# Hybrid decoder block on one core: first weights split in three, a third raw-weight buffer, later squares

## The chip, the cores and the metric

One NeuronCore of one Trainium2 chip runs the whole kernel in one launch. The metric is the device time of one execution in microseconds (us); the number for the kernel before is the median of three executions. One further execution was recorded by the hardware profiler, and every row below comes from that one.

## What is computed

The reference is one decoder block (batch 1, 512 tokens, model width 1024, depth 1). The whole change lies in its first lines, the first norm and the first columns of the combined projection:

```python
h = rms_norm(x, attn_norm_g[i])
u = h @ w_in[i]
u_sb, u_rw, u_gate = jnp.split(u, [SB_COLS, SB_COLS + RW_COLS], axis=-1)
q, k, v = jnp.split(u_sb.reshape(bsz, seq, 3 * SB_HEADS, SB_HEAD_DIM), 3, axis=2)
o_sb = stick_breaking_attention(q, k, v).reshape(bsz, seq, SB_WIDTH)
o_rw = rwkv7_time_mix(u_rw, ...)
```

After it come the gated merge of the two branches, a squared-ReLU MLP, the gated per-layer embedding and a final norm. All inputs and outputs are float32.

## The kernel before

**Numbers in two halves.** Products keep float32 accuracy by splitting each operand in a rounded high part and the low rest: `x = hi + lo`. A product is then three matmuls (`mm3`, lines 186 to 194): weight-hi by x-hi (L191), weight-hi by x-lo (L192), weight-lo by x-hi (L193), each 128 contraction rows by 512 tokens. The split of a weight tile costs one cast on ScalarE (ACT) for `w_hi` and one subtraction on VectorE (DVE) for `w_lo`: lines 221 and 222 for the very first tiles, 175 and 176 for all later ones.

**Weights in units.** All weights lie in memory as units of 128 x 1024 float32 (512 KB). The list `seq` fixes the order in which they are used. `load_to` (L157 to L162) starts a unit's load from the SyncE queue (SP) into a raw buffer `w_raw`, of which there are two; a buffer comes free when the subtraction that makes `w_lo` has read it. `fetch_to` then issues the cast and the subtraction into one of three pairs `w_hi`, `w_lo`; a pair comes free when TensorE (PE) has done the last matmul with it. Units are counted from 0 here: units 0 and 1 are the first q and k columns (head pair 0), unit 2 the first v columns, units 3 to 5 those of head pair 1, and so on.

**The start.** PE first runs matmuls on a zeroed tile `warm` (L335, L336) whose result nobody reads. Meanwhile x, transposed to eight tiles of 128 features by 512 tokens (256 KB each), comes in; `first_x(k)` (L349 to L355) loads tile k, scales it by the norm's gain into `h_hi` on ACT (L353) and makes `h_lo` on DVE (L354). The gain lies in `cols`, a small table of per-feature vectors. `first_weights` (L344 to L347) loads and splits a part of unit 0 or 1. The first loop on PE (L528 to L530) goes over the eight tiles k and for each does six matmuls, three with unit 0 and three with unit 1: 48 in all. Then comes the v projection (24 matmuls, unit 2), and after it the projections of head pair 1 (24 each).

**The norm comes late.** The division by the root mean square is not applied to x but to the results: `sum_squares` (L224 to L234) squares each x tile on ACT and adds it up in `ssum` on DVE; one float32 matmul with a constant matrix sums over partitions (L263, within `rstd_of`), and ACT and DVE turn that into `rs` (L251 to L258). `projected` multiplies q, k and v by `rs` on DVE (`qT` L394, `kT` L406, `vT` L414) and splits them; PE transposes `vT` (L421) and multiplies q with k (`scores`, L458 to L460). So the first scores wait for `ssum`, L263, `rs`, `qT` and the splits of q and k, in that order.

**What sets the order.** A scheduler puts the instructions in order for each engine at build time; on the chip each engine keeps that order. `tc.issue_after(i)` pins what is issued inside it behind instruction i on the same engine. DMA loads share eight completion semaphores: a load that reuses one waits in the queue until the load before it on that semaphore has landed.

Of the kernel before, what the change touches and what calls it, by code (L numbers as in the profile page):

```python
# [10 lines left out]
F32 = mybir.dt.float32  # L11
F32R = mybir.dt.float32r
BF16 = mybir.dt.bfloat16
AF = mybir.ActivationFunctionType
# [4 lines left out]
P = 128  # L19
T = 512  # L20
D = 1024
KT = D // P
# [63 lines left out]
def tile_block(ctx: ExitStack, tc: tile.TileContext, xT, xt, pT, wts, lora, cols_d, gfin_d, consts_d, out, dbg=None):  # L86
    nc = tc.nc
    act, dve, pool, pe, sync = nc.scalar, nc.vector, nc.gpsimd, nc.tensor, nc.sync
# [17 lines left out]
    cols = const.tile([P, NCOLS], F32, name="cols")  # L106
# [12 lines left out]
    def col(name, i):  # L119
        return cols[:, COLS[name] + i:COLS[name] + i + 1]  # L120
# [35 lines left out]
    def load_to(n):  # L156
        while len(loaded) < min(n, len(seq)):  # L157
            i = len(loaded)
            loaded.append(None)
            if seq[i][0] != U_FF2:  # L160
                loaded[i] = wpool.tile([P, 1024], F32, name="w_raw", bufs=2)
                sync.dma_start(out=loaded[i], in_=unit(i))  # L162

    def fetch_to(n, ahead=0):
# [59 lines left out]
    def sum_squares(pool_, src, k, ssum):  # L224

        if k == 0:
            act.activation(out=ssum, in_=src, func=AF.Square)
            return
        sq = pool_.tile([P, T], F32, name="sq", bufs=2)[:, 0:src.shape[-1]]
        act.activation(out=sq, in_=src, func=AF.Square)  # L230
        if k == 1:
            dve.scalar_tensor_tensor(out=ssum, in0=sq, scalar=NORM_EPS * D / P, in1=ssum, op0=ALU.add, op1=ALU.add)
        else:
            dve.tensor_tensor(out=ssum, in0=ssum, in1=sq, op=ALU.add)  # L234
# [42 lines left out]
    with ExitStack() as sA:  # L277
# [43 lines left out]
        with ExitStack() as s1:  # L321
# [10 lines left out]
            warm = p1.tile([P, T], BF16, name="warm", tag="sp")  # L332
            pool.memset(warm, 0.0)
            ps = ps_z()
            for _ in range(12):  # L335
                pe.matmul(ps, warm[:, 0:P], warm, start=True, stop=True)  # L336
            sync.dma_start(out=cols, in_=cols_d)
            ssum = p1.tile([P, T], F32, name="ssum", tag="wl")

            raws = [wpool.tile([P, 1024], F32, name="w_raw", bufs=2) for _ in range(2)]  # L340
            first_w = [[wpool.tile([P, 1024], F32R, name=n) for n in ("w_hi", "w_lo")] for _ in range(2)]
            xs_in = {}

            def first_weights(i, part):  # L344
                cs = slice(part * 512, part * 512 + 512)
                sync.dma_start(out=raws[i][:, cs], in_=unit(i)[:, cs])
                split(first_w[i][0][:, cs], first_w[i][1][:, cs], raws[i][:, cs])  # L347

            def first_x(k):  # L349
                x_in = p1.tile([P, 2, T], F32, name="x_in", tag=("sp", "sph", "spl", "wh")[k // 2]) if k % 2 == 0 else xs_in[k - 1][0]  # L350
                sync.dma_start(out=x_in[:, k % 2, :], in_=xT[:, k, :])
                xs_in[k] = x_in, x_in[:, k % 2, :]
                act.activation(out=h_hi[:, k, :], in_=xs_in[k][1], func=AF.Copy, scale=col("attn_g", k))  # L353
                dve.scalar_tensor_tensor(out=h_lo[:, k, :], in0=xs_in[k][1], scalar=col("attn_g", k), in1=r32(h_hi[:, k, :]),  # L354
                                         op0=ALU.mult, op1=ALU.subtract)  # L355


            first_weights(0, 0)
            first_x(0)
            first_weights(1, 0)  # L360
            for k in range(1, 4):
                first_x(k)
            first_weights(0, 1)
            first_weights(1, 1)
            for k in range(4, KT):
                first_x(k)
            loaded.extend(raws)
# [2 lines left out]
                ready[seq[i]] = [tuple(first_w[i])]  # L370
            fetch_to(3)

            for k in range(KT):
                sum_squares(p1, xs_in[k][1], k, ssum)
            sync.dma_start(out=cst, in_=consts_d[:, 0:NCONST])
            first = p1.tile([P, 4 * P], F32, name="first", tag="sums", bufs=1)
            sync.dma_start(out=first, in_=consts_d[:, NCONST:NCONST + 4 * P])
# [1048 lines left out]
```

## Time and profile before

| what | value |
|---|---|
| median of three executions | 870.2 us (869.28 to 870.54) |
| the profiled execution, its own time | 869.75 us |
| its span, first to last instruction | 867.7 us |
| PE busy in the span | 851.4 us (98%) |
| DVE busy | 678.1 us (78%) |
| ACT busy | 448.6 us (52%) |
| loads of weight units, median from issue to landing | 3.5 us |
| loads of x tiles, median from issue to landing | 5.7 us |

The profile lists every instruction with its engine, source line, start and duration. A timeline merges neighbours of one line: "x3" is three instructions, and the second number then spans all of them. What stands in square brackets is the idle time of the engine just before, and what ended it. PE matmuls are pipelined: one of 512 columns is listed with about 0.39 us, but the next one starts about 0.23 us after it, so the pace is read from start to start, or from the count in a window. SPq and PEq are the queues that issue for an engine. Idle time of an engine that nobody waits for costs nothing.

### The profile page before, as it was taken

The numbers are of one execution on the slowest core, as the hardware profiler recorded it, in microseconds if no ns is written. First come the engines' busy times: TensorE is split into PE (matmuls) and PEld (weight loads), VectorE is DVE, ScalarE is ACT, GpSimd is POOL, SyncE is SP. The second block draws the span as 40 slices with busy tenths as digits, with TensorE's granted clock in tenths as the row PEclk, the third lists the DMA queues.
The fourth block names the chain that finished last, engine by engine and source line by source line (L and its number), as shares of the span: only waits on it lengthen the run. The fifth ranks groups of instructions, "written<-read, shape, count | busy, mean of one in ns | idle before, by whom it ended". The sixth has DMA issues, their size and how long they took to land.

```text
span 867.7 us, 13424 instructions
## 1 busy us (share of the span) xinstructions
PE 851.4 (98%) x5182; PEld 686.8 (79%) x5182; DVE 678.1 (78%) x1228; ACT 448.6 (52%) x703; POOL 80.4 (9%) x138
## 2 busy tenths in 40 slices
PE   8999999999999999999999999999999999999996
PEld 5778787877777777777888888888888888888885
DVE  7899987896979888776754789858985987697767
ACT  6888887744335343534424464344434543453744
POOL 1432431002302111020000000000000000000000
PEclk9999999999999999999999999999999999999999
DMA  7212212221121224437935621531252034300422
GB/s 269 98 49 66 82 62 85 74 97 51 62 87 57 80 73 153 141 116 258 318 121 181 232 73 38 182 120 49 83 184 98 25 127 164 98 1 0 170 73 98
DMA packets 32272, 95.32 MB, mean 110 GB/s; under 512 B 3664, under 2 KB 3664, under 8 KB 32208
## 3 DMA queue, kind: packets, MB, share of 16 engines
q1 hardware_dynamic: 32208, 94.46, 32.6%
q8 instruction: 41, 0.67, 0.3%
q14 instruction: 23, 0.19, 0.1%
HBM read 83.96 MB, written 10.49 MB: 109 GB/s over the span
## 4 chain that ended last, share of the span: by engine, by line
PE 81%; DVE 10%; ACT 4%; issue 1%; DMA 1%; SPq 0%; POOL 0%; POOLq 0%; DVEq 0%; ACTq 0%
PE ps_m L191 13%; PE ps_m L193 13%; PE ps_m L192 13%; PE ps_m L206 9%; PE ps_m L207 9%; PE ps_m L208 9%; DVE w_lo L176 2%; PE ps_g L817 1%; PE ps_o L497 1%; PE ps_g L193 1%; PE ps_c L935 1%; PE ps_s L944 1%; PE ps_g L191 1%; PE ps_g L192 1%; PE ps_g L906 1%
## 5 line engine op out<-in xcount | busy, mean ns | idle before, releaser
L175 ACT CAST w_hi<-w_raw 128x1024 fp32r<-128x1024 f32 x94 | 99.0, 1053 | 170.4 <-PE ps_m L192 110.8
L176 DVE TENSOR_TENSOR w_lo<-w_raw,w_hi 128x1024 fp32r<-128x1024 f32 x94 | 115.1, 1225 | 37.6 <-ACT w_hi L175 37.2
L191 PE MATMUL ps_m<-h_hi,w_hi 128*128 128x512 f32 x320 | 130.6, 410 | 0.9 <-ACT h_hi L353 0.9
L192 PE MATMUL ps_m<-h_lo,w_hi 128*128 128x512 f32 x320 | 128.0, 400 | 0.0
L193 PE MATMUL ps_m<-h_hi,w_lo 128*128 128x512 f32 x320 | 127.5, 399 | 0.0
L191 PE MATMUL ps_m<-hx,w_hi 128*128 128x512 f32 x256 | 99.6, 390 | 0.4 <-ACT hx L1049 0.4
L192 PE MATMUL ps_m<-hx,w_hi 128*128 128x512 f32 x256 | 99.6, 390 | 0.0
L193 PE MATMUL ps_m<-hx,w_lo 128*128 128x512 f32 x256 | 99.5, 389 | 0.0
L191 PEld LDWEIGHTS ps_m<-h_hi,w_hi 128*128 128x128 f32 x320 | 60.7, 190 | 11.4 <-ACT h_hi L353 1.6
L193 PEld LDWEIGHTS ps_m<-h_hi,w_lo 128*128 128x128 f32 x320 | 60.3, 188 | 11.8
L192 PEld LDWEIGHTS ps_m<-h_lo,w_hi 128*128 128x128 f32 x320 | 60.5, 189 | 11.0 <-DVE h_lo L354 1.1
L191 PEld LDWEIGHTS ps_m<-hx,w_hi 128*128 128x128 f32 x256 | 48.0, 188 | 10.5 <-ACT hx L1049 0.6
L192 PEld LDWEIGHTS ps_m<-hx,w_hi 128*128 128x128 f32 x256 | 48.1, 188 | 10.2 <-DVE hx L1050 0.2
L193 PEld LDWEIGHTS ps_m<-hx,w_lo 128*128 128x128 f32 x256 | 48.0, 188 | 10.0
L207 PE MATMUL ps_m<-w_lo,fS 128*128 128x512 f32 x128 | 49.8, 389 | 0.0
L208 PE MATMUL ps_m<-w_hi,fS 128*128 128x512 f32 x128 | 49.8, 389 | 0.0
L206 PE MATMUL ps_m<-w_hi,fS 128*128 128x512 f32 x128 | 49.8, 389 | 0.0
L1291 POOL TENSOR_SCALAR r<-s 128x1 f32<-128x1 f32 x1 | 0.5, 519 | 478.9 <-DVE t L1271 478.9
L208 PE MATMUL ps_m<-w_hi,fA 128*128 128x512 f32 x96 | 37.4, 389 | 0.0
L207 PE MATMUL ps_m<-w_lo,fA 128*128 128x512 f32 x96 | 37.3, 389 | 0.0
L206 PE MATMUL ps_m<-w_hi,fA 128*128 128x512 f32 x96 | 37.3, 389 | 0.0
L221 ACT CAST fS<-sums 128x256 fp32r<-128x256 f32 (+1 forms) x32 | 19.8, 620 | 33.3 <-DVE sums L1141 33.3
(378 smaller groups left out, 1911.6 us busy)
## 6 DMA issues: line engine op xcount, KB each, us to landing
w_raw<-in_wts_dram SPq DMA_DIRECT2D x98, 512.0 KB, 3.5
gates<-gg SPq DMA_DIRECT2D x16, 256.0 KB, 2.1
x_in<-in_xT_dram SPq DMA_DIRECT2D x8, 256.0 KB, 5.7
tmp<-gates SPq DMA_DIRECT2D x8, 256.0 KB, 4.0
upsb<-tmp SPq DMA_DIRECT2D x8, 256.0 KB, 3.5
ga<-upsb SPq DMA_DIRECT2D x8, 256.0 KB, 5.4
gb<-gates SPq DMA_DIRECT2D x8, 256.0 KB, 5.4
xs<-in_xt_dram SPq DMA_DIRECT2D x4, 512.0 KB, 5.9
```

The lines of the kernel that those rows point to most:

```text
L175: act.copy(out=hi, in_=raw)
L176: dve.tensor_tensor(out=lo, in0=raw, in1=r32(hi), op=ALU.subtract)
L191: pe.matmul(ps, wh, xh[:, k, t], start=first, stop=False)
L192: pe.matmul(ps, wh, xl[:, k, t], start=False, stop=False)
L193: pe.matmul(ps, wl, xh[:, k, t], start=False, stop=last)
L206: pe.matmul(ps, xh[:, k + j], wh, start=first and j == 0, stop=False, skip_group_check=True)
L207: pe.matmul(ps, xh[:, k + j], wl, start=False, stop=False, skip_group_check=True)
L208: pe.matmul(ps, xl[:, k + j], wh, start=False, stop=last and j == 1, skip_group_check=True)
L221: act.copy(out=hi, in_=src)
L497: pe.matmul(ps_o[:, j * P:T], vv[:, j, hh, :, :].rearrange("p a d -> p (a d)"), part[:, ZB[j]:ZB[j] + ZN[j]], start=j == 2 and part is wh, ...
L817: last = pe.matmul(ps[rows, k], left[rows, k, :], rhs[rows, k], start=True, stop=True)
L906: pe.matmul(ps[:, j * P:(j + 1) * P], Z[:, hh * 4 + g * 2 + cp, :], MA[:, g * 4 + j, :], start=True, stop=True)
```

## The change

The diff, whole but for the moved line numbers:

```diff
@@ load_to
-                loaded[i] = wpool.tile([P, 1024], F32, name="w_raw", bufs=2)
+                loaded[i] = wpool.tile([P, 1024], F32, name="w_raw", bufs=3)
@@ start of the attention stage
-            for _ in range(12):
+            for _ in range(9):
                 pe.matmul(ps, warm[:, 0:P], warm, start=True, stop=True)
-            sync.dma_start(out=cols, in_=cols_d)
+            act.dma_start(out=cols, in_=cols_d)
-            raws = [wpool.tile([P, 1024], F32, name="w_raw", bufs=2) for _ in range(2)]
+            raws = [wpool.tile([P, 1024], F32, name="w_raw", bufs=3) for _ in range(2)]
-            xs_in = {}
-
-            def first_weights(i, part):
-                cs = slice(part * 512, part * 512 + 512)
+            xs_in, tiles = {}, []
+
+            def first_weights(i, lo, n):
+                cs = slice(lo * P, (lo + n) * P)
                 sync.dma_start(out=raws[i][:, cs], in_=unit(i)[:, cs])
                 split(first_w[i][0][:, cs], first_w[i][1][:, cs], raws[i][:, cs])
@@ first_x
-                act.activation(out=h_hi[:, k, :], in_=xs_in[k][1], func=AF.Copy, scale=col("attn_g", k))
+                with tc.issue_after(tiles[-1]) if tiles else nullcontext():
+                    tiles.append(act.activation(out=h_hi[:, k, :], in_=xs_in[k][1], func=AF.Copy, scale=col("attn_g", k)).ins)
@@ the order of the first loads
-            first_weights(0, 0)
+            first_weights(0, 0, 2)
             first_x(0)
-            first_weights(1, 0)
-            for k in range(1, 4):
-                first_x(k)
-            first_weights(0, 1)
-            first_weights(1, 1)
+            first_weights(1, 0, 2)
+            first_x(1)
+            first_x(2)
+            for i in range(2):
+                first_weights(i, 2, 2)
+            first_x(3)
+            for i in range(2):
+                first_weights(i, 4, 4)
             for k in range(4, KT):
                 first_x(k)
@@ the squares
-            for k in range(KT):
-                sum_squares(p1, xs_in[k][1], k, ssum)
+            for k, behind in enumerate((0, 4, 5, 6, 7, 7, 7, 7)):
+                with tc.issue_after(tiles[behind]):
+                    sum_squares(p1, xs_in[k][1], k, ssum)
@@ kernel
-    nc = bacc.Bacc("TRN2", target_bir_lowering=False, num_devices=1)
+    nc = bacc.Bacc("TRN2", target_bir_lowering=False, num_devices=1, dynamic_dma_scratch_size=2048)
```

In words: three warm matmuls fewer; `cols` is loaded from ACT's queue; units 0 and 1 come in parts of 256, 256 and 512 columns (two, two and four tiles k) instead of two halves; the scaling of tile k is pinned behind that of tile k-1 on ACT, and the squares of tiles 1 to 7 behind the scalings of tiles 4 to 7; a third raw buffer, for which a smaller DMA scratch leaves the room. The output is the same function of the inputs.

Line numbers behind line 350 move up, by 1 at `h_hi` and `h_lo` and by 5 from the squares on. On every engine the order of instructions differs in the first 60 us; behind that PE's is the same, instruction for instruction, and the others differ in a few neighbours.

The loads on the SP queue, from the first on (`w_raw` at L346 are parts of units 0 and 1, `w_raw` at L162 whole units from unit 2 on, `x_in` the tiles of x):

Before:

```order
L337 DMA cols<-in_cols_dram 128x74
L346 DMA w_raw<-in_wts_dram 128x512
L351 DMA x_in<-in_xT_dram 128x512
L346 DMA w_raw<-in_wts_dram 128x512
L351 DMA x_in<-in_xT_dram 128x512 x3
L346 DMA w_raw<-in_wts_dram 128x512 x2
L351 DMA x_in<-in_xT_dram 128x512 x4
L162 DMA w_raw<-in_wts_dram 128x1024
L375 DMA cst<-in_consts_dram 128x584
L377 DMA first<-in_consts_dram 128x512
L162 DMA w_raw<-in_wts_dram 128x1024
```

Now:

```order
L346 DMA w_raw<-in_wts_dram 128x256
L351 DMA x_in<-in_xT_dram 128x512
L346 DMA w_raw<-in_wts_dram 128x256
L351 DMA x_in<-in_xT_dram 128x512 x2
L346 DMA w_raw<-in_wts_dram 128x256 x2
L351 DMA x_in<-in_xT_dram 128x512
L346 DMA w_raw<-in_wts_dram 128x512 x2
L351 DMA x_in<-in_xT_dram 128x512 x4
L162 DMA w_raw<-in_wts_dram 128x1024
L380 DMA cst<-in_consts_dram 128x584
L382 DMA first<-in_consts_dram 128x512
L162 DMA w_raw<-in_wts_dram 128x1024 x3
```

`cols` is gone from this queue, the quarters let x tiles 0 to 2 in with half the weight bytes ahead of them, and the load of unit 3 (the second whole unit) now has the loads of units 4 and 5 right behind it, ahead of `lora_w`.

The subtractions and the norm on DVE, where `rs` is made and q, k and v are scaled (`w_lo` at L176 here are units 3 to 5). Before:

```order
L540 CAST caus_b<-first 128x128
L176 TENSOR_TENSOR w_lo<-w_raw,w_hi 128x1024 x2
L256 SCALAR_TENSOR_TENSOR nt<-nt,ps_z 128x512
L257 SCALAR_TENSOR_TENSOR rs<-nt,rs 128x512
L176 TENSOR_TENSOR w_lo<-w_raw,w_hi 128x1024
L394 SCALAR_TENSOR_TENSOR qT<-ps_m,rs 128x512
L406 TENSOR_TENSOR kT<-ps_m,rs 128x512
L414 TENSOR_TENSOR vT<-ps_z,rs 128x512
```

Now:

```order
L176 TENSOR_TENSOR w_lo<-w_raw,w_hi 128x1024
L234 TENSOR_TENSOR ssum<-ssum,sq 128x512
L176 TENSOR_TENSOR w_lo<-w_raw,w_hi 128x1024 x2
L256 SCALAR_TENSOR_TENSOR nt<-nt,ps_z 128x512
L257 SCALAR_TENSOR_TENSOR rs<-nt,rs 128x512
L399 SCALAR_TENSOR_TENSOR qT<-ps_m,rs 128x512
L411 TENSOR_TENSOR kT<-ps_m,rs 128x512
L419 TENSOR_TENSOR vT<-ps_z,rs 128x512
```

The subtraction of unit 5 stood between `rs` and `qT`; it now stands ahead of `nt`. All eight squares are still added up ahead of it.

The end of the fourth projection on PE (unit 3, into `ps_z`), the transposes of `vT` and the first scores (L458, now L463). Before:

```order
L191 MATMUL ps_z<-h_hi,w_hi 128x512
L421 MATMUL ps_m<-cst,vT 128x128 x4
L192 MATMUL ps_z<-h_lo,w_hi 128x512
L193 MATMUL ps_z<-h_hi,w_lo 128x512
L191 MATMUL ps_z<-h_hi,w_hi 128x512
L192 MATMUL ps_z<-h_lo,w_hi 128x512
L193 MATMUL ps_z<-h_hi,w_lo 128x512
L191 MATMUL ps_m<-h_hi,w_hi 128x512
L458 MATMUL ps_z<-qq_271,kk_281 128x256
```

Now:

```order
L193 MATMUL ps_z<-h_hi,w_lo 128x512
L426 MATMUL ps_m<-cst,vT 128x128 x4
L191 MATMUL ps_m<-h_hi,w_hi 128x512
L192 MATMUL ps_m<-h_lo,w_hi 128x512
L193 MATMUL ps_m<-h_hi,w_lo 128x512
L191 MATMUL ps_m<-h_hi,w_hi 128x512
L192 MATMUL ps_m<-h_lo,w_hi 128x512
L193 MATMUL ps_m<-h_hi,w_lo 128x512
L463 MATMUL ps_z<-qq_274,kk_284 128x256
```

The transposes moved behind the last five matmuls of the fourth projection, and six matmuls of the fifth (into `ps_m`) stand ahead of the first scores where one stood. In the same way the matmul of `ssum` (L263) moved from behind the 7th to behind the 19th of the 24 matmuls of the v projection.

## Rows read from the trace of the kernel before

**Rows 1.** The page: the span, and busy time of each engine

```profile
span 867.7 us, 13424 instructions
...
PE 851.4 (98%) x5182; PEld 686.8 (79%) x5182; DVE 678.1 (78%) x1228; ACT 448.6 (52%) x703; POOL 80.4 (9%) x138
```

**Rows 2.** Windows of 20 and 50 us: us, busy of PE, PEld, DVE, ACT, POOL, clock, DMA

```profile
40.00:60.00 20.00, 19.73 (x103) 15.63 (x102) 18.52 (x36) 16.62 (x33) 5.01 (x11) 1.00 0.16 53
...
400.00:450.00 50.00, 50.00 (x223) 41.39 (x222) 34.39 (x45) 21.11 (x29) 0.00 (x0) 1.00 0.68 231
```

**Rows 3.** Short windows at the start, same columns

```profile
1.30:6.40 5.10, 5.09 (x13) 1.98 (x13) 1.56 (x3) 2.60 (x5) 2.07 (x4) 1.00 0.76 239
...
9.00:12.00 3.00, 3.00 (x13) 2.32 (x14) 3.00 (x5) 3.00 (x6) 0.00 (x0) 1.00 0.94 353
```

**Rows 4.** What PE waited for: us in total, times, longest

```profile
PE ps_m L191 <- ACT h_hi L353: 0.9, 1, 0.9
...
PE ps_o L497 <- DVE wl L512: 0.7, 2, 0.5
```

**Rows 5.** Timeline of PE at the start: start, us, engine, line, what

```profile
1.31 5.30 PE L336 MATMUL ps_z<-warm 128*128 128x512 bf16 x12 [1.31 <-POOL warm L333]
6.05 0.99 PE L191 MATMUL ps_m<-h_hi,w_hi 128*128 128x512 f32 x1
6.84 0.48 PE L192 MATMUL ps_m<-h_lo,w_hi 128*128 128x512 f32 x1
```

**Rows 6.** Timeline of the SP queue, its first loads

```profile
0.74 0.39 SPq L337 DMA_DIRECT2D cols<-in_cols_dram  x1
1.18 0.42 SPq L346 DMA_DIRECT2D w_raw<-in_wts_dram  x1
1.65 0.42 SPq L351 DMA_DIRECT2D x_in<-in_xT_dram  x1
...
4.97 3.48 SPq L351 DMA_DIRECT2D x_in<-in_xT_dram  x4
12.19 0.33 SPq L162 DMA_DIRECT2D w_raw<-in_wts_dram  x1
```

**Rows 7.** Timeline of ACT, 0 to 20 us

```profile
0.73 1.28 ACT L124 ACT_TABLE_LOAD   x1 [0.73 <-PEq L1418]
4.16 0.62 ACT L221 CAST w_hi<-w_raw 128x512 fp32r<-128x512 f32 x1 [2.15 <-DMA w_raw<-in_wts_dram]
5.13 0.72 ACT L353 ACTIVATE h_hi<-x_in,cols 128x512 fp32r<-128x512 f32 x1 [0.36 <-DMA x_in<-in_xT_dram]
...
8.13 0.72 ACT L353 ACTIVATE h_hi<-x_in,cols 128x512 fp32r<-128x512 f32 x1 [1.24 <-DMA x_in<-in_xT_dram]
```

**Rows 8.** Timeline of DVE, 0 to 20 us

```profile
2.62 0.36 DVE L538 TENSOR_SCALAR omm<-cols 128x14 f32<-128x14 f32 x1 [2.62 <-DMA cols<-in_cols_dram]
```

**Rows 9.** Timeline of PE, 20 to 62 us

```profile
20.80 1.07 PE L263 MATMUL ps_z<-ssum,cst 128*128 128x512 f32 x2
...
30.43 0.66 PE L421 MATMUL ps_m<-cst,vT 128*128 128x128 f32 x4 [0.35 <-DVE vT L414]
...
32.65 0.36 PE L458 MATMUL ps_z<-qq,kk 128*128 128x256 f32 x1 [0.17 <-DVE kk L410]
```

**Rows 10.** Timeline of DVE, 20 to 62 us

```profile
20.00 0.69 DVE L234 TENSOR_TENSOR ssum<-ssum,sq 128x512 f32<-128x512 f32 x1
...
25.99 0.69 DVE L257 SCALAR_TENSOR_TENSOR rs<-nt,rs 128x512 f32<-128x512 f32 x1
27.35 1.23 DVE L176 TENSOR_TENSOR w_lo<-w_raw,w_hi 128x1024 fp32r<-128x1024 f32 x1 [0.67 <-ACT w_hi L175]
28.49 0.68 DVE L394 SCALAR_TENSOR_TENSOR qT<-ps_m,rs 128x512 f32<-128x512 f32 x1
...
37.23 0.41 DVE L222 TENSOR_TENSOR spl<-sp,sph 128x256 fp32r<-128x256 f32 x1
```

**Rows 11.** Timeline of ACT, 20 to 62 us

```profile
26.27 1.05 ACT L175 CAST w_hi<-w_raw 128x1024 fp32r<-128x1024 f32 x1 [1.63 <-DMA w_raw<-in_wts_dram]
```

## The prediction, made before the changed kernel ran

> **What bounds the kernel now.** I read the page first, then the windows, then what PE waited for, then the start and the stretch to the first scores engine by engine. The page says that PE is busy for 851.4 of 867.7 us [rows 1], so at most some 16 us of idle time are there to be won anywhere. The windows say where they are not: from 400 us on whole windows of 50 us are full on PE, while in the attention stage PE has 19.73 of 20 us, DVE 18.52 and ACT 16.62 [rows 2]. So a stage that starts earlier hands on its gain as long as PE is the fullest engine, but DVE stands close behind it. The list of PE's waits is short: 0.9 us for an x tile at the start and some tenths in the attention stage [rows 4].
>
> The start is where the change works. The twelve warm matmuls begin at 1.31 and the first useful one is listed at 6.05 and the second follows only at 6.84 [rows 5]. Twelve warm ones take 5.30 us, 0.44 each; 512 columns at TensorE's lower level, 1.2 GHz, are 0.427 (the granted clock column says 1.00 there all the same [rows 3], so I go by the pace). From 9 to 12 us it is 13 starts in 3.00 us, 0.23 each [rows 3], and 50 / 223 = 0.224 where PE is full [rows 2]: the upper level, 2.4 GHz. I reckon with 0.227. The first useful matmul is listed with 0.99 us and the second with 0.48 [rows 5], so I put the rise near 7.0 us. The twelfth warm matmul runs until 1.31 + 12 x 0.427 = 6.43; the x tile was scaled at 5.13 + 0.72 = 5.85 [rows 7]. So the warm matmuls, not the data, held the first useful one, by some 0.5 us. Then PE starves: x tile 1 reaches ACT only at 8.13, after 1.24 us of waiting [rows 7].
>
> The first loop has 48 matmuls, 48 x 0.227 = 10.9 us at the upper pace. L263 starts at 20.80 [rows 9] behind 7 matmuls of the v projection, so the loop ended its turn at 20.80 - 7 x 0.227 = 19.2. From 6.05 that is 13.2 us, so about 2.3 us are lost to the low clock and to late tiles. This and the 0.9 us ahead of it is what the change can win at the start.
>
> **Part by part.**
>
> *Three warm matmuls fewer.* PE is free at 1.31 + 9 x 0.427 = 5.15 instead of 6.43.
>
> *`cols` on ACT's queue, quarters of weights.* SP's issues are 0.47 us apart [rows 6]; x tile 0 is issued at 1.18 instead of 1.65, with 128 KB ahead of it instead of 293 KB. At the 239 to 353 GB/s of the start [rows 3] those 165 KB are 0.5 to 0.7 us. It came by 5.07 (ACT took it at 5.13 after a wait [rows 7]), so now by 3.9 to 4.1. `cols` took 1.9 us from its issue at 0.74 to its first reader at 2.62 [rows 6, 8]. No row shows a load issued from ACT. If its queue runs on during the table load at 0.73 [rows 7], `cols` lands at about 2.6; if it waits for it, it is issued at 2.0 and lands at 3.9, and a transfer that shares with the others might take 1 us more, 4.9. I take 3.9, the same load behind the table load. Then `h_hi` of tile 0 is done at about 4.1 + 0.72 = 4.8 to 4.9, and the first useful matmul starts at 5.15, held by the warm ones. With 4.9 it would start at 5.7; that end costs 0.5.
>
> *Splitting itself.* Four narrow casts and subtractions stand in place of two wide ones. A 256-wide subtraction takes 0.41 us [rows 10], a 512-wide cast 0.62 [rows 7]; so ACT and DVE each get 4 x 0.41 - 2 x 0.62 = 0.4 us more work, or nothing if narrow ones cost half. Idle time of both engines ahead of 8.1 us covers it; without that cover it would cost the 0.4.
>
> *The loop.* Quarters let k = 0 and k = 1 start on 512 and 768 KB instead of 805 and 1061. So PE has 12 matmuls (about 3.5 us, four of them at the lower pace) to do before it needs tile 2, where it had 6 before it starved. Three squares, each about as long as a cast, no longer stand between the scalings on ACT. Never starved, the loop would end at 5.15 + 4 x 0.427 + 44 x 0.227 = 16.8. Tile 2 and the second quarters can still come late as tile 1 did; I give that 0.5, so 17.3, 1.9 us earlier than now; starved as badly as now (2.1 us lost) it is 18.2, 1.0 earlier.
>
> *The third buffer.* Unit 2 is loaded at 12.19 today, when the subtraction of unit 0's second half frees its buffer [rows 6]; now it goes right behind x tile 7 (today issued by 4.97 + 3.48 = 8.45 [rows 6]). Nothing on PE waits for it today, so this wins nothing by itself: it keeps unit 2 ready for a PE that comes 1.9 us sooner. It counts once more at unit 5, whose cast waits for its load until 26.27 [rows 11]; now that load is in by then. From 33 us on, casts wait for PE and loads for casts, and an earlier load is hidden.
>
> *Squares later, L263 later.* L263 now stands behind 19 instead of 7 matmuls: 17.3 + 19 x 0.227 = 21.6, against 20.80. The last addition to `ssum` ends at 20.7 today [rows 10]; it now has one more subtraction of a unit ahead of it, but no idle time, about 20.9, so PE still meets it ready. From L263's start to the end of `rs` are 26.68 - 20.80 = 5.9 us [rows 9, 10]; so `rs` comes at 27.5 instead of 26.7, 0.8 later. But unit 5's subtraction (27.35 to 28.58) no longer stands between `rs` and `qT` (28.49) [rows 10]. So `qT` starts at 27.5, **1.0 us earlier**. That is the gain of the chain through DVE and ACT.
>
> PE meets it like this: after L263 come 5 + 24 matmuls, 21.6 + 0.5 + 29 x 0.227 = 28.7; the transposes wait for `vT`, 27.5 + 0.6 + 0.6 + 0.7 = 29.4, a wait of 0.7 where 0.35 stands today [rows 9]. The first scores come 4.2 us behind `qT` today (28.49 to 32.65 [rows 9, 10]), so at 31.7, with five more matmuls of the fifth projection done. PE is ahead by 0.95 + 5 x 0.227 = **2.1 us** there, the chain by 1.0.
>
> **The sum.** The end moves by between 1.0 (if the attention stage runs at DVE's pace) and 2.1 (if at PE's). The fullest engine there is PE, with 19.73 against 18.52 [rows 2], so I take 1.8, near PE's end. Against the profiled execution's own 869.75 us (span 867.7 [rows 1] and 2.05 around it) that is 867.95; this execution lies 0.45 under the median of the three, so on the median's scale 870.2 - 1.8 = **868.4 us**. Behind 60 us nothing moves on PE, and the few swaps of neighbours on ACT, DVE and SP are hidden by a full PE.
>
> **The rivals.**
>
> 1. *DVE takes it back.* PE comes earlier to scores that come only 1.0 us earlier or less, and the waits for `wl` and `vT` [rows 4, 9] grow by the rest. For it: DVE's 18.52 of 20 us. Against it: 1.5 us idle per 20 us on DVE, spent waiting for others that now come sooner. Gain 0 to 1.1, about 869.6.
>
> 2. *The clock rises later.* With nine warm matmuls PE's unbroken work ends at 5.15, and what follows has gaps. The rows show only that PE had been busy from 1.31 without a gap when the upper pace came, shortly after the twelfth. Each matmul at the lower pace costs 0.20 us more. The loop ends as late as today once (19.2 - 16.8) / 0.20 = 12 more of the 48 run low, that is, when the rise comes behind 5.15 + 16 x 0.427 = 12 us. A rise midway to that, 6 more low matmuls, ends the loop at 18.0 and leaves 869.1; with half the loop low (20 more) it ends at 20.8, 1.6 later than today, 871.8: the case on the slower side. The Trainium skill (TensorE: Matmul & The Clock Gate, on the HAM clock gate) speaks for this rival: there sustained activity releases the clock, and the moment varies from run to run because the monitor does not start with the kernel; by that the rise is an open number in each run. The one trace here has it once, near 7.0, so it cannot show whether that holds.
>
> 3. *More than the sum.* All tiles come in time, and the attention stage's waits shrink too [rows 4]. Gain 2.6 or more, 867.3 and less.
>
> 4. *The new loads do nothing.* x tile 1 was late by itself: it reached ACT 3 us behind tile 0 [rows 7] with 512 KB between them, 170 GB/s where the windows have 239 to 353 [rows 3]. If the same delay hits tile 1 again, the loop ends near 18.2 and the gain is 1.0, 869.2.
>
> **How the numbers follow.** Forecast 0.56 (its own range 867.3 to 869.2), rival 1 0.16, rival 2 0.10 (0.04 of it slower than before), rival 3 0.11, rival 4 0.07. One measurement of this kernel can tell about 0.2% from no change, 1.74 us, so the bound lies at 868.5. Faster by more than that: a little over half of the forecast (0.34) and rival 3 (0.11), 0.45. Slower: rival 2's slow part, 0.04, and 0.01 for the swaps of neighbours. Within: the rest, 0.50. The range leaves out the far part of rival 3 and the slower cases: 866.7 to 870.1.
>
> **What would show it.** Right: first useful matmul near 5.2 instead of 6.05; L263 near 21.6; `qT` near 27.5; scores near 31.7; PE's timeline behind 150 us shifted by 1 to 2 us and otherwise the same. Wrong: a first `h_hi` behind 5.2 with `cols` as its releaser; matmuls at 0.43 us a start after 7.5; longer waits for `vT`, `wh`, `wl`; a shift at 60 us that is gone at 140.

## The result: 0.42% slower, and the profile after

The changed kernel takes 874.17 us (median of 7 runs, 870.97 to 874.72), the kernel before 870.12 on the same chip (7 runs, 869.28 to 870.54). The ratio is 1.0042, 95% interval 1.0031 to 1.0052: slower, where 868.4 was forecast. The profiled run of the changed kernel is its longest, 874.72 us. The page:

```profile
span 872.7 us, 13433 instructions
...
PE 852.6 (98%) x5179; PEld 686.9 (79%) x5179; DVE 679.9 (78%) x1230; ACT 449.7 (52%) x705; POOL 80.4 (9%) x138
```

PE's busy time is up by 1.2 us and the span by 5.0 [rows 1]: most of the loss is idle time of PE. To find its places I subtracted, for every matmul, its start before from its start after. The difference is -0.15 us at 56 us and still -0.10 at 142, then +1.6 at 155, +1.6 at 298, +4.9 at 315, +5.1 from 360 to the end. So there are three stories: a start that keeps almost nothing, a loss at 144 us and a loss at 301 us. The last two lie where the prediction had said that nothing moves.

**The start.** PE's timeline in the changed kernel (start, us, engine, line, what), then ACT's and DVE's:

```profile
1.31 3.58 PE L336 MATMUL ps_z<-warm 128*128 128x512 bf16 x9 [1.31 <-POOL warm L333]
4.73 0.49 PE L191 MATMUL ps_m<-h_hi,w_hi 128*128 128x512 f32 x1
...
22.20 1.02 PE L263 MATMUL ps_z<-ssum,cst 128*128 128x512 f32 x2
...
32.25 0.35 PE L463 MATMUL ps_z<-qq,kk 128*128 128x256 f32 x1 [0.19 <-DVE kk L415]
```

```profile
0.76 0.40 ACTq L337 DMA_DIRECT2D cols<-in_cols_dram  x1
...
3.96 0.72 ACT L354 ACTIVATE h_hi<-x_in,cols 128x512 fp32r<-128x512 f32 x1 [0.42 <-DMA x_in<-in_xT_dram]
...
6.85 0.72 ACT L354 ACTIVATE h_hi<-x_in,cols 128x512 fp32r<-128x512 f32 x1 [1.21 <-DMA x_in<-in_xT_dram]
```

```profile
21.28 0.69 DVE L234 TENSOR_TENSOR ssum<-ssum,sq 128x512 f32<-128x512 f32 x1
...
27.36 0.69 DVE L257 SCALAR_TENSOR_TENSOR rs<-nt,rs 128x512 f32<-128x512 f32 x1
28.09 0.69 DVE L399 SCALAR_TENSOR_TENSOR qT<-ps_m,rs 128x512 f32<-128x512 f32 x1
```

The first useful matmul comes at 4.73 instead of 6.05 [rows 5], L263 at 22.20 instead of 20.80 [rows 9], `qT` at 28.09 instead of 28.49 [rows 10], the first scores at 32.25 instead of 32.65 [rows 9]. The gain of the chain is thus 0.4 us, and two stops of PE at 49 and 51 us, at which it waits for DVE, take PE's lead back (the kernel before waits once there, for 0.16 us). The window of 20 us stands beside them, and one from 300 us that is used below:

```profile
49.77 0.50 PE L502 MATMUL ps_o<-wh,vv 128*128 128x512 f32 x1 [0.52 <-DVE wh L516]
...
51.20 0.50 PE L502 MATMUL ps_o<-wl,vv 128*128 128x512 f32 x1 [0.48 <-DVE wl L517]
```

```profile
40.00:60.00 20.00, 19.01 (x100) 15.05 (x98) 19.21 (x37) 16.25 (x33) 6.38 (x12) 1.00 0.16 54
...
300.00:310.00 10.00, 8.05 (x196) 5.87 (x191) 6.39 (x14) 3.56 (x6) 0.00 (x0) 0.83 0.17 64
```

From 40 to 60 us DVE is now the fuller engine, 19.21 against PE's 19.01; before it was 18.52 against 19.73 [rows 2].

**144 us.** Here DVE copies a constant into `X`, a working tile of the second branch (`rwkv7_time_mix`), and POOL clears tiles of the same branch. DVE and then POOL in the kernel before:

```profile
144.29 0.20 DVE L836 COPY X<-cst 128x64 f32<-128x64 f32 x1 [3.14 <-DMA o_sb<-oo]
144.40 0.68 DVE L304 TENSOR_TENSOR u<-ps_m,rs 128x512 f32<-128x512 f32 x1
145.00 1.22 DVE L176 TENSOR_TENSOR w_lo<-w_raw,w_hi 128x1024 fp32r<-128x1024 f32 x1
```

```profile
144.48 0.53 POOL L581 MEMSET keep<- 128x512 f32 x1 [15.59 <-DVE X L836]
```

and in the changed kernel:

```profile
144.29 2.44 DVE L841 COPY X<-cst 128x64 f32<-128x64 f32 x1 [3.25 <-DMA o_sb<-oo]
144.40 2.33 DVE L304 TENSOR_TENSOR u<-ps_m,rs 128x512 f32<-128x512 f32 x1
145.00 1.73 DVE L176 TENSOR_TENSOR w_lo<-w_raw,w_hi 128x1024 fp32r<-128x1024 f32 x1
```

```profile
144.36 0.53 POOL L586 MEMSET keep<- 128x512 f32 x1 [15.56 <-issue]
...
145.72 0.96 POOL L601 MEMSET Z<- 128x1024 f32 x1
146.74 1.10 POOL L617 MEMSET lxl<- 64x512 f32 x2
```

A copy of 0.20 us takes 2.44, and ends at 146.73: in the 0.06 us between POOL's memset of Z, done at 146.68, and its next one. `u` and the subtraction behind it start when they did before (144.40 and 145.00) and end at 146.73 as well. The subtraction alone takes 1.22 us, so by the rows DVE worked on at its pace and the end of all three came late; DVE's next product starts at 146.81 instead of 146.25. `u` is late by 1.65 us, with it ACT's next step, and PE stands 1.7 us back by 155.

Copy and memset wait for the same DMA semaphore, which comes near 144.2 in both kernels (the transfer `o_sb<-oo` in the rows). The transfers are dealt to other semaphores now: the memset stands behind six DMA semaphores instead of seven, and behind the one that comes last POOL has one more semaphore instruction to pass instead of two. So the memset starts 0.12 us earlier, on top of the copy instead of at its end.

**301 us.** Here PE has runs of 64 matmuls of 32 rows by 32 or 64 columns, tiny ones, back to back. PE in the kernel before, then in the changed one:

```profile
298.91 1.10 PE L817 MATMUL ps_g<-LX,LB 32*32 32x64 f32 x64
299.94 0.50 PE L192 MATMUL ps_m<-h_lo,w_hi 128*128 128x512 f32 x1
```

```profile
300.52 0.85 PE L822 MATMUL ps_g<-LX,LB 32*32 32x64 f32 x42
303.32 0.53 PE L822 MATMUL ps_g<-LX,LB 32*32 32x64 f32 x22 [1.95 <-issue]
...
306.49 0.80 PE L191 MATMUL ps_m<-h_hi,w_hi 128*128 128x512 f32 x1
```

Of 64 tiny matmuls 42 run, then PE stands for 1.95 us and waits for nothing that the profile shows ("issue"); 1.36 us after it goes on the granted clock falls to its lower level, 1.2 GHz, from 304.68 to 308.10 (hence 0.83 in the window above). The DMA queues give a hint. From 290 to 300 us the kernel before has a packet on the queue that brings instructions, the changed kernel has none there, and one from 300 to 302. One row of each:

```profile
q8 instruction: 1, 0.02, 0.9%
```

```profile
q8 instruction: 1, 0.02, 2.9%
```

Over the run this queue has 41 packets of 16 KB in either kernel; PE executes 10,459 instructions before and 10,451 now (matmuls, weight loads and semaphore instructions in order of time), and at 256 to a packet that is 41. Counted from 0, the instruction that PE stops ahead of is number 4289.

### The profile page after: what moved, and what is told of

It is laid out like the page before. It is cut to its first block, busy times and chain, and to the rows that moved or that the text cites. A ratio compares the mean times of both kernels' runs of the same rounds, so it can differ in the third digit from the quotient of the medians.

```text
span 872.7 us, 13433 instructions
## 1 busy us (share of the span) xinstructions
PE 852.6 (98%) x5179; PEld 686.9 (79%) x5179; DVE 679.9 (78%) x1230; ACT 449.7 (52%) x705; POOL 80.4 (9%) x138
## 4 chain that ended last, share of the span: by engine, by line
PE 82%; DVE 10%; ACT 5%; issue 2%; DMA 1%; SPq 0%; POOL 0%; POOLq 0%; DVEq 0%; ACTq 0%
PE ps_m L191 13%; PE ps_m L193 13%; PE ps_m L192 13%; PE ps_m L208 9%; PE ps_m L206 9%; PE ps_m L207 9%; DVE w_lo L176 1%; PE ps_g L822 1%; PE ps_o L502 1%; PE ps_g L193 1%; PE ps_g L192 1%; PE ps_g L191 1%; PE ps_g L911 1%; PE ps_c L940 1%; DVE LX L843 1%
## 5 line engine op out<-in xcount | busy, mean ns | idle before, releaser
L176 DVE TENSOR_TENSOR w_lo<-w_raw,w_hi 128x1024 fp32r<-128x1024 f32 x94 | 115.8, 1232 | 33.6 <-ACT w_hi L175 33.1
```

Source lines behind the costliest of these rows:

```text
L176: dve.tensor_tensor(out=lo, in0=raw, in1=r32(hi), op=ALU.subtract)
```

## The experiments

Three theories, with their rivals:

- **F:** 4289 is the border of a packet. The fetch of the next packet starts ahead of a border, at a place that the program has to reach; the changed kernel's program is seven instructions shorter there (three matmuls, their weight loads, one semaphore instruction), which puts this place behind the wait for `own8`, a tile that DVE makes, at the head of a run of tiny matmuls. So the fetch starts only with the run, and 256 instructions of it take only 2.3 us. Rival C: transfers or chance, whatever the program's length.
- **P:** a copy on DVE and memsets on POOL exclude each other. Rival Q: DVE waits for something else.
- **S:** the later squares cost the start its gain. Rival L: the quarters of loads or the third buffer do.

The table has the median and the ratio to the kernel before on the same chip (10 or 11 runs against 31 to 33, the changed kernel 7 against 7). Then, from the one profiled run of each, it has the start of the same matmuls against the kernel before (us, minus is earlier), at 56, 142, 180, 298, 315 and 500 us. The last column is the number of the first instruction of the tiny matmuls near 297 us (4019 before, 4012 in the changed kernel).

| run | us | ratio, 95% | 56 | 142 | 180 | 298 | 315 | 500 | number |
|---|---|---|---|---|---|---|---|---|---|
| changed | 874.17 | 1.0042 (1.0031 to 1.0052) | -0.15 | -0.10 | +1.57 | +1.61 | +4.87 | +5.12 | 4012 |
| pad | 870.86 | 1.0014 (1.0004 to 1.0023) | +0.17 | +0.17 | +1.66 | +1.74 | +1.73 | +1.47 | 4020 |
| before9 | 873.20 | 1.0036 (1.0020 to 1.0051) | -1.03 | -0.99 | -1.08 | -1.06 | +0.70 | +0.28 | 4013 |
| xt_act | 871.86 | 1.0021 (1.0011 to 1.0031) | +0.18 | +0.21 | +0.12 | +0.12 | +3.47 | +3.07 | 4012 |
| xt_tt | 872.03 | 1.0029 (1.0017 to 1.0040) | -0.25 | -0.21 | -0.21 | -0.20 | +1.18 | +1.19 | 4012 |
| pad_xt | 869.37 | 0.9994 (0.9985 to 1.0004) | -0.20 | -0.19 | -0.29 | -0.27 | -0.27 | -0.51 | 4020 |
| px_sq | 868.80 | 0.9991 (0.9981 to 1.0000) | -1.20 | -0.72 | -0.78 | -0.76 | -0.74 | -0.11 | 4021 |
| px_buf2 | 869.05 | 1.0000 (0.9987 to 1.0013) | -0.33 | -0.31 | -0.44 | -0.42 | -0.44 | +3.35 | 4020 |
| b9pad | 869.97 | 1.0002 (0.9992 to 1.0011) | +1.71 | +1.72 | +1.74 | +1.72 | +1.69 | +1.58 | 4021 |
| b9pad_buf3 | 868.99 | 0.9993 (0.9982 to 1.0003) | -0.29 | -0.29 | -0.40 | -0.42 | -0.44 | -0.80 | 4022 |
| b_sq | 869.92 | 1.0001 (0.9992 to 1.0010) | -0.35 | -0.29 | -0.01 | -0.03 | -0.04 | -0.14 | 4018 |
| best1 | 868.68 | 0.9990 (0.9982 to 0.9999) | -1.37 | -0.87 | -0.38 | -0.37 | -0.38 | -0.80 | 4019 |
| b2_buf2sq | 869.84 | 1.0002 (0.9993 to 1.0011) | +1.25 | +1.30 | +1.31 | +1.36 | +1.35 | +0.96 | 4019 |

**pad**: the changed kernel, its program made one instruction longer than before.

```diff
+            for _ in range(4):
+                pe.matmul(ps[:, 0:8], warm[:, 0:P], warm[:, 0:8], start=True, stop=True)
             for _ in range(9):
```

> Four matmuls of 8 columns stand before the nine warm ones, so that TensorE's program again has as many instructions ahead of the tiny matmuls at 300 us as the kernel before (one more). Theory F (the stop of 2.0 us between two tiny matmuls at 301.2 us is a late fetch of the program's next 16 KB, late because six instructions fewer put its trigger behind the wait of the burst's first instruction, and the clock falls because of the stop): no stop above 0.5 us there, no half clock at 305 us, an instruction packet near 296 us, and 3.3 us less than the changed kernel's profiled 874.7: 870.9 to 871.6. Rival C (the stop is a collision with transfers or a whim of the chip, whatever the program's length): the stop is there again, 873.5 to 874.7. The 1.7 us at 144 us are lost by both.

Measured 870.86, and PE's run of 64 is whole:

```profile
300.65 1.10 PE L824 MATMUL ps_g<-LX,LB 32*32 32x64 f32 x64
```

The step at 301 us is gone, the step at 144 us is there. An instruction packet comes at 296.20. Theory F holds; that a certain place in the program starts the fetch is inferred from such rows, no run moved it by itself.

**before9**: the kernel before, its program made shorter by six instructions.

```diff
-            for _ in range(12):
+            for _ in range(9):
```

> The kernel before with nine warm matmuls instead of twelve and nothing else. Theory F: the program is six instructions shorter as in the changed kernel, so the stop of about 2 us in the tiny matmuls near 300 us appears here too, and a fall of the clock may follow: 871.8 to 873.5, though the start is no later. Rival C (the stop has to do with the transfers of the changed kernel): no stop, 869.3 to 870.3. At 144 us nothing is lost by either, VectorE's copy into X takes 0.2 us.

```profile
297.85 0.85 PE L817 MATMUL ps_g<-LX,LB 32*32 32x64 f32 x42
300.53 0.53 PE L817 MATMUL ps_g<-LX,LB 32*32 32x64 f32 x22 [1.83 <-issue]
```

The same stop, ahead of the same instruction, 4289, in a kernel that has no other part of the change: rival C falls. The clock did not fall in the profiled run (870.12 us), but runs reach 876.13 with a mean clock of 0.991 to 0.997. And PE stood 1.0 us ahead from 33 to 298 us. That can't be put down to the three warm matmuls: the first useful matmul came later than before, at 6.60, for want of `h_hi`, and 0.7 of the lead is unit 5's weights, which came in time (`rs` 25.61, `qT` 27.45, against 25.99 and 28.49 [rows 10]).

**xt_act** and **xt_tt**: the changed kernel with the first copy into `X` done by ScalarE, or by VectorE in another form, as the larger of the constant and itself (`s8b` stands for the broadcast view of the constant).

```diff
-                dve.tensor_copy(out=Xt, in_=s8b)
+                (act.copy if hp == 0 else dve.tensor_copy)(out=Xt, in_=s8b)
```
```diff
+                if hp == 0:
+                    dve.tensor_tensor(out=Xt, in0=s8b, in1=s8b, op=ALU.max)
+                else:
                     dve.tensor_copy(out=Xt, in_=s8b)
```

> The changed kernel with the first copy into X (the one that took 2.4 us at 144.3 us) done by ScalarE instead of VectorE. Theory P (that copy and GpSimd's chain of memsets exclude each other, and with one wait fewer GpSimd comes first): VectorE's next product u is done by 145.1 us, and the step from 144 to 152 us costs 0 to 0.3 us instead of 1.7: 1.4 to 1.7 us less than the changed kernel, with the stop at 301 us still there: 872.4 to 873.4. Rival Q (VectorE waits there for something else, a transfer or a semaphore that the profile puts on the copy): VectorE stands until 146.7 us as before, ScalarE's copy takes 0.2 us, and the time stays at 874 to 874.7.

> The changed kernel with its first copy into X still on VectorE, at the same place behind the same waits, but as the larger of the constant and itself (a tensor_tensor of two SBUF inputs) instead of a copy. Theory P (a VectorE copy and a GpSimd memset exclude each other by the form of the copy): it starts at 144.2 to 144.4 us and takes 0.15 to 0.4 us instead of 2.4, the product u behind it is done by 145.2 us, and the step from 144 to 152 us costs 0 to 0.4 us instead of 1.7. Rival Q (VectorE waits for something else than the port until 146.7 us, such as the buffer that X is written to): it lasts until 146.7 us in this form too. The stop of 2 us in the tiny matmuls, at the 193rd of 256 instructions, stays in either case: 871.5 to 873.4 by P, 873 to 874.7 by Q.

Both lose nothing at 144 us and keep the stop at 301, as P and F said; 871.86 lies under what was expected of xt_act, 872.03 within that of xt_tt. In xt_act ScalarE did its copy only at 148.8 us, behind the memsets, so it shows that DVE was the victim but not of what. In xt_tt the instruction stands on DVE in the same place, and POOL's memset starts 0.07 us behind it as before. DVE, then POOL:

```profile
144.01 0.23 DVE L843 TENSOR_TENSOR X<-cst 128x64 f32<-128x64 f32 x1 [3.09 <-DMA o_sb<-oo]
144.16 0.68 DVE L304 TENSOR_TENSOR u<-ps_m,rs 128x512 f32<-128x512 f32 x1
```

```profile
144.08 0.53 POOL L586 MEMSET keep<- 128x512 f32 x1 [15.41 <-issue]
```

0.23 us instead of 2.44 by the form alone: Q falls. The Trainium skill (SBUF — State Buffer, Who interferes with whom) has the rule: a copy on VectorE can run in a mode that takes the port pair shared with GpSimd, a tensor_tensor has no such mode and, with two inputs in SBUF, meets only GpSimd instructions that read; whoever comes second is blocked entirely. The rows agree, with two things more: the copy, though listed 0.07 us ahead of the first memset, is the one that lost, and its end came not behind one memset of 0.5 us but behind nine in a row. How close the race is shows in b9pad_buf3, below, where the copy is as it was before and has a lead of 0.10 us: there it takes its 0.20 us, and the memset on top of it 0.56 instead of 0.53.

```profile
143.96 0.20 DVE L838 COPY X<-cst 128x64 f32<-128x64 f32 x1 [3.11 <-DMA o_sb<-oo]
```

```profile
144.06 0.56 POOL L583 MEMSET keep<- 128x512 f32 x1 [15.47 <-DMA o_sb<-oo]
```

**pad_xt**: both repairs (pad and xt_act).

> Both edits together: the four short matmuls and the copy into X on ScalarE. Theories F and P: neither loss is left and what the start still has at 56 us (0.1 us) and a little at 300 us stays: 869.4 to 870.0, which is 0.1 to 0.7 us under the kernel before. If P falls alone: 871 to 871.6. If F falls alone: 872.4 to 873.4. If both fall: 874.

869.37, level with the kernel before. The two losses are the whole of the slowdown, and what is left of the change is worth nothing that these runs can tell. Why, the next four ask.

**b9pad**: before9 with the four short matmuls of pad.

> The kernel before with nine warm matmuls and four of 8 columns ahead of them, so that the program's length ahead of the tiny matmuls stays. With nine warm matmuls alone TensorE stood 1.04 us ahead of the kernel before from 33 us to 298 us and lost it in the stop. Theory F (only the length brought that stop): no stop above 0.5 us near 300 us, 1.0 us ahead to the end: 868.3 to 868.9, 0.1% under the kernel before. Rival C (fewer warm matmuls lead to the stop or to a fall of the clock in another way): stop or fall again, 870.5 to 873.

No stop at 301 us, as F said, but 869.97 is a miss: 868.3 to 868.9 was expected. The profiled run stands 1.7 us behind at 56 us where before9 stood 1.0 ahead: PE waited 0.96 us for `h_hi` and 1.37 us for `w_hi`, and its clock, which had risen at 4.11, was at the lower level from 7.52 to 14.35.

```profile
8.70 0.80 PE L191 MATMUL ps_m<-h_hi,w_hi 128*128 128x512 f32 x1 [1.37 <-ACT w_hi L221]
```

```profile
5.00:15.00 10.00, 7.53 (x19) 5.41 (x20) 7.19 (x12) 8.19 (x15) 0.00 (x0) 0.66 0.80 280
```

Its runs spread from 868.55 to 871.32, those of the kernel before beside it from 868.49 to 872.24. So with the old loads fewer warm matmuls gain nothing that the runs show, and one profile of such a start tells little: rival C is right here in so far as the clock can fall by another way.

**px_sq**: pad_xt with the squares as in the kernel before, and without the pin of each scaling behind the one before it (the cut leaves out the edits of pad and xt_act).

```diff
-                with tc.issue_after(tiles[-1]) if tiles else nullcontext():
+                with nullcontext():
...
-            for k, behind in enumerate((0, 4, 5, 6, 7, 7, 7, 7)):
-                with tc.issue_after(tiles[behind]):
-                    sum_squares(p1, xs_in[k][1], k, ssum)
+            for k in range(KT):
+                sum_squares(p1, xs_in[k][1], k, ssum)
```

> pad_xt with the squares put where the kernel before has them. Theory S (the later squares let the scheduler put both ql parts of the second pair of heads ahead of the 512-wide product sp on VectorE, and so bring the two stops of 0.7 us at 49 and 50 us): neither stop, and TensorE at 56 us 0.7 to 1.3 us ahead of the kernel before (pad_xt: 0.2): 868.2 to 868.9. Rival L (the quarters of loads and the third buffer bring them): both stops are there, 0 to 0.3 us ahead at 56 us, 869.2 to 869.7. Neither expects a stop at 300 us or at 144 us.

868.80, PE 1.20 us ahead at 56 us (0.7 of it is left at 142), no stop at 49 to 51. DVE in pad_xt, then in px_sq:

```profile
28.00 0.69 DVE L401 SCALAR_TENSOR_TENSOR qT<-ps_m,rs 128x512 f32<-128x512 f32 x1
...
36.48 1.49 DVE L409 TENSOR_TENSOR ql<-qT,qq 64x512 fp32r<-64x512 f32 x2
38.00 0.69 DVE L473 SCALAR_TENSOR_TENSOR sp<-ps_z,sp 128x512 f32<-128x512 f32 x1
```

```profile
24.53 0.69 DVE L400 SCALAR_TENSOR_TENSOR qT<-ps_m,rs 128x512 f32<-128x512 f32 x1
...
33.25 0.69 DVE L472 SCALAR_TENSOR_TENSOR sp<-ps_z,sp 128x512 f32<-128x512 f32 x1
...
36.86 1.39 DVE L408 TENSOR_TENSOR ql<-qT,qq 64x512 fp32r<-64x512 f32 x2
```

Left where they were, the squares let `qT` come 3.5 us earlier and the 512-wide `sp` 4.8. Together with the pin of the scalings the later squares were a loss of 1.0 us at 56 us in these two profiles, as S said; by whole runs (868.80 and 869.37) the two kernels are not clear of each other. Which of the two pins it is, and whether it acts by the order of `ql` and `sp` or by the late `qT`, this run does not part.

**px_buf2**: pad_xt with two raw buffers and the old scratch. **b9pad_buf3**: b9pad with three and the small scratch.

> pad_xt with two buffers for raw weights and the DMA scratch of the kernel before. Theory S (the squares set VectorE's order, the third buffer does not): the stops at 49 and 50 us are there, 869.2 to 869.8, as pad_xt within 0.3 us. Rival L (the earlier loads of the third buffer disturb the first pairs of heads): no stops, 0.7 us or more ahead at 56 us, 868.3 to 868.8. If the third buffer was of use, its load comes late and it is slower: above 870.2.

> b9pad with the third buffer and the smaller scratch, nothing else. Theory S: the third buffer takes away ScalarE's wait for the raw weights of unit 2 (1.63 us at 26 us in the kernel before, on no path) and changes nothing that TensorE waits for: within 0.3 us of b9pad, 868.1 to 868.9. Rival L: it costs 0.7 us or more at 45 to 52 us: 869.2 to 870.

px_buf2 keeps both stops (0.55 and 0.48 us, in pad_xt 0.56 and 0.47) and its median, 869.05, lies 0.3 us under pad_xt's, about as S said. Its profiled run shows the border again, 5 x 256 = 1280 instructions further on, at 5569, with a fall of the clock behind it (357.08 to 363.91):

```profile
354.19 0.59 PE L824 MATMUL ps_g<-LX,LB 32*32 32x32 f32 x45 [0.25 <-DVE LX L870]
355.93 0.38 PE L824 MATMUL ps_g<-LX,LB 32*32 32x32 f32 x19 [1.15 <-issue]
```

px_sq stops ahead of 5569 too, for 0.88 us, with no fall. b9pad_buf3 loses nothing at 45 to 52 us, so L falls, but it is 1.0 us faster than b9pad where S had said at most 0.3. Its `qT` follows 0.72 us behind `rs`, in b9pad 1.79, with unit 5's subtraction between them (the wait that the expectation lays to unit 2 is unit 5's): with the squares where they were, the buffer seems to be worth something. The ranges of the two overlap (868.03 to 870.57 against 868.55 to 871.32), and b9pad's profiled run had its slow start, so this pair alone does not show it.

**b_sq**: the kernel before with the later squares and the pin of the scalings alone.

> The kernel before with the later squares alone. Theory S: both ql parts come ahead of the 512-wide sp on VectorE as in the changed kernel, TensorE stops by 0.7 us twice at 49 to 51 us, and what the start brings or loses, it leaves 56 us later than the kernel before by 0.3 us or more: 869.8 to 871. Rival L (the quarters of loads are needed for that loss): no stops at 49 to 51 us and 0 to 1 us ahead at 56 us: 868.5 to 869.5. No stop at 300 us by either (the program has the length of the kernel before, less one).

A miss for S: DVE has the order of the changed kernel, but the stops at 49.79 and 50.79 us are of 0.23 and 0.21 us only (one of 0.51 us at 37 comes with them), PE stands 0.35 us ahead at 56, and the time is the same as before, 869.92. So the order by itself costs nothing; that it hurts where the start is otherwise earlier fits px_sq, but no run varied the start alone.

**best1**: the changed kernel with all three repairs: the squares as in px_sq (both pins gone), the copy as in xt_tt, and the length now without extra matmuls, by twelve warm ones of 384 columns (this edit is shown). **b2_buf2sq**: best1 with two raw buffers and the old scratch.

```diff
-            for _ in range(9):
-                pe.matmul(ps, warm[:, 0:P], warm, start=True, stop=True)
+            for _ in range(12):
+                pe.matmul(ps[:, 0:384], warm[:, 0:P], warm[:, 0:384], start=True, stop=True)
```

> The changed kernel with three repairs: squares as in the kernel before, the first copy into X as a tensor_tensor, and twelve warm matmuls of 384 columns in place of nine of 512 (as many columns, but the program's length of the kernel before). By theories F, P and S together it is px_sq without its four short matmuls: no stop at 300 us, nothing lost at 144 us, 0.7 to 1.2 us ahead at 56 us: 868.3 to 868.9 where the kernel before has 869.5, a ratio of 0.9985 to 0.9995. If one of the three falls, 870 or more. A stop of 1 us at 354 us may remain, as in px_sq.

> best1 with two buffers for raw weights and the DMA scratch of the kernel before: what is left of the change is the warm matmuls, the constants on ScalarE's queue and the quarters of weights. If the third buffer is worth nothing by itself (theory S): within 0.4 us of best1, 868.2 to 869.2. If unit 5's weights come too late without it: the wait of 1.6 us of ScalarE at 26 us is back and it is slower by 0.5 us or more.

best1 takes 868.68, ratio 0.9990 (0.9982 to 0.9999): level with px_sq and just faster than the kernel before. b2_buf2sq is 1.2 us slower (its fastest run takes 869.38, eight of best1's eleven take less): the third buffer is of use there. `qT` in best1, then in b2_buf2sq, which has unit 5's subtraction ahead of it again:

```profile
24.32 0.69 DVE L398 SCALAR_TENSOR_TENSOR qT<-ps_m,rs 128x512 f32<-128x512 f32 x1
```

```profile
25.12 1.22 DVE L176 TENSOR_TENSOR w_lo<-w_raw,w_hi 128x1024 fp32r<-128x1024 f32 x1
26.26 0.68 DVE L398 SCALAR_TENSOR_TENSOR qT<-ps_m,rs 128x512 f32<-128x512 f32 x1
```

Of the 1.9 us between these two `qT`, 0.7 arose before the buffer can act (ACT got x tile 1 at 7.25 instead of 6.55, best1 issues unit 2 at 8.50); about 1.0 is the subtraction. ScalarE's wait of 1.6 us at 26 us, named as the sign, did not come back. The expectation that the buffer is worth nothing by itself was wrong there: it holds in px_buf2, where the squares are late.

## Why the prediction was wrong

**The step that failed** is the sentence "Behind 60 us nothing moves on PE and the few swaps of neighbours on ACT, DVE and SP are hidden by a full PE". Of the 5.1 us between the two profiled runs, 1.7 arise at 144 us and 3.3 at 301 us. The repairs part them by whole runs as well: pad lies 1.3 us above the kernel before on its chip where the changed kernel lay 4.05 above it on its own, so the border with its fall of the clock cost 2.7; xt_act and xt_tt lie 2.3 above, so the copy cost 1.7. I had compared the orders of the engines and found them nearly equal, but neither loss is one of order: one is a semaphore instruction fewer ahead of a memset, the other seven instructions fewer ahead of a border. The prediction gave the swaps of neighbours a chance of 0.01 to make the kernel slower and named no other cause behind 60 us.

The other steps, in the prediction's order:

- *Three warm matmuls fewer*: right in kind, and in the profiled run better than said by luck: 4.73 where 5.15 stood, because the clock rose at 4.31 while they ran. xt_act and xt_tt have the same start, instruction for instruction; there the clock rose at 5.21 and 6.26, and the first useful matmul came at 5.23 and 5.48. Rival 2 (a later rise) did not come; over the 14 profiles the first rise lies between 4.11 and 6.98, the latest being that of the kernel before. In b9pad it was the fall behind it that cost. The Trainium skill's statement that the moment differs from run to run (TensorE: Matmul & The Clock Gate, the HAM clock gate) is borne out by these three starts.
- *`cols` on ACT's queue*: issued at 0.76, while the table loads, so the queue runs on, as the favourable end of the bound had it. `h_hi` of tile 0 starts at 3.96 (4.1 forecast), in xt_act and xt_tt at 4.45 and 4.71, inside the bound.
- *The loop*: x tile 1 came late again (a wait of 1.21 where 1.24 stood [rows 7]), as rival 4 had it; the loop ended at 22.20 - 19 x 0.227 = 17.9 instead of 17.3, within its bounds.
- *The third buffer*: unit 5's subtraction left the gap between `rs` and `qT`, as said. In px_buf2 it is there again, and the time is the same; with the squares left alone the buffer was worth 1.2 us (best1 against b2_buf2sq).
- *Squares later*: the price was too low. L263 came at 22.20 (21.6 forecast), its last addition ended at 21.28 + 0.69 = 21.97 (20.9), `qT` came at 28.09 (27.5): a gain of 0.4 for the chain instead of 1.0 (`rs` ended 1.4 us later than before, 0.8 forecast). And the question not asked was where the chain would be with the squares left alone: `qT` at 24.53 in px_sq.
- *The sum*: I took 1.8, near PE's end. Rival 1 came: DVE was the fuller engine from 40 to 60 us and took PE's lead back but for 0.15 us. That step alone would have left 870, no change; best1, with the squares left alone, has 1.37 us at 56 us, inside the forecast's 1.0 to 2.1, but 0.87 at 142, 0.38 at 180 and 0.80 at 500: what the start wins is not handed on whole, as the prediction's first paragraph had it.

What is shown: the border (before9 alone makes the stop, pad alone removes it), the copy (xt_tt), the two pins of squares and scalings together, at 56 us: the six profiles with the changed start and both pins (changed, pad, xt_act, xt_tt, pad_xt, px_buf2) lie between -0.33 and +0.18 there, px_sq and best1 at -1.20 and -1.37. By b2_buf2sq that gain needs the third buffer: without it that profile lies at +1.25, a part of which is its late x tile. What is not shown: how the pins do it, since b_sq has them on the old start and loses nothing; and why a stop is followed by a fall of the clock in some runs. Of the six profiles with a stop of 0.88 us or more ahead of 4289 or 5569 three have a fall within 1.4 us of its end (changed, xt_act, px_buf2); the other three and the eight profiles without such a stop have none between 15 and 860 us. The stop comes first, but what decides was not tried.

## What to carry to other kernels

When a change shortens one engine's program, or moves semaphores, look beyond the rows that it touches: find the runs of tiny instructions and count at which of them the instruction packets end, and look for pairs of instructions on DVE and POOL that start within a tenth of a microsecond of each other. Before work is put off because the engine ahead is not waiting for it, ask what would come earlier if it stayed. And take a start's gain as won only where the next stage's fullest engine has room for it.

## What the runs showed of the hardware that was not expected

- PE's program comes in packets of 256 instructions, and a run of tiny matmuls outruns them. Every stop of this kind lies ahead of instruction 4289 or 5569, which differ by 5 x 256. For 4289 the four kernels whose run of tiny matmuls begins at 4012 or 4013 all stop, by 1.42 to 2.01 us; the ten at 4018 to 4022 do not. The packet starts at 293.5 to 296.4 us in all ten, 2.1 us or more ahead of the run, and at 298.07 to 301.06 in the four, 1.8 to 2.4 us into it; there PE goes on 1.2 to 1.6 us after the packet has landed. The Trainium skill (Runtime: NRT & Kernel Launch, Instruction fetch mechanics) has the blocks of 16 KiB and 256 instructions and calls the cost of a border mostly hidden; the packets agree, the stops are where it isn't hidden.
- Four matmuls of 8 columns (0.27 us in all in b9pad's start), or twelve warm ones of 384 columns instead of nine of 512, move a run of tiny matmuls against such a border.
- A 64-column copy on DVE stood 2.4 us behind nine memsets on POOL when it had a lead of 0.07 us, and took its 0.20 us when it had 0.10 (b9pad_buf3); the same values written by a tensor_tensor took 0.23 us. The two instructions behind the copy started on time and ended with it.
